# The first item of the gate projection ahead of the last Strassen product

## The chip, the core and the metric

The kernel runs on one core of a Trainium2 chip. The metric is the device time of one execution in microseconds (us), lower is better. The core has a matmul engine (PE, with its weight loads as PEld), a vector engine (DVE), a scalar engine (ACT), GpSimd (POOL) and a queue for DMA issues (SP). Each engine works its own instructions in the order in which the program lists them and waits for the others by semaphores.

## What is computed

One decoder layer on a sequence of 1024 tokens with 1024 channels, all in float32. What matters here is the order of the stages:

```python
h = layer_norm(x)
u, b_gate, c_gate, z_a, z_s, xbc, dt_raw, g_a, g_s = split(h @ w_in)     # the large projection
y_a = silu(z_a) * b_gate * causal_conv3(c_gate * u)
y_a = y_a @ w_a_out                                                      # "a" items
y_s = gated_group_rmsnorm(ssd(xbc, dt) + d_skip * xs, z_s) @ w_s_out     # "s" items
mixed = sigmoid(g_a) * y_a + sigmoid(g_s) * y_s
h = layer_norm(alpha * h + mixed @ w_o)
```

## The kernel before

Every product is made from float32 split in a high and a low part (`hi`, `lo`), as three matmuls: hi by hi, hi by lo, lo by hi. A row group is a block of 128 rows of the transposed input weight, so 128 output channels. The large projection takes two row groups at a time as a pair, and makes each pair by seven products of half size (a Strassen scheme); the pairs are numbered 0 to 43, the products 1 to 7. The last pairs, 40 to 43, hold the gates g_s.

The work of PE is one list, `items`, written out by hand, and one loop over it (L1069) issues each item with all that belongs to it on the other engines. An item `("p", p, j)` is product j of pair p: 12 matmuls of 128x512, four slices of the inner dimension by three. An item `("a", j, kh)` is half of the inner dimension of output block j of the gate projection (`y_a @ w_a_out`, whose result is multiplied by sigmoid(g_a)): 24 matmuls, 12 into each of two PSUM banks. The items `("s", g, j)` follow. Within a pair the products come as 1, 2, 6, 5, 7, 4, and product 3 is put off until after product 1 of the next pair. After the last pair there is no next one, so its product 3 stands right behind its product 4, and then the `a` items begin.

The loop prepares weights ahead: at item n ACT makes the `hi` of item n+3 (`prep_hi`, L288), DVE the `lo` of item n+2 (`prep_lo`, L105 by way of `sub_split`), and SP loads raw weights up to item n+5. `lo` tiles have three buffers and `hi` tiles four, so each waits until PE is through with an older item. PSUM results are added up one item later: what `sums` holds for item n+1 is put on DVE behind the weight preparation of that item (L1029). Everything from item 21 on is pinned: each engine keeps the order in which the loop wrote it.

Three banks matter. Products 5 and 3 of a pair accumulate in the bank `c4`, in one tile. Between the two, DVE has to add the partial sum to the second row group (`add(obh, C4[p], obl)` of product 7, one item later); product 3 may only begin after that. Product 4 uses the bank `cx`, and DVE empties it by `add(obl, ps, obl)` one item later. `pbank` gives the `a` items their banks in turn, and the first that it gives, to the item ("a", 0, 0), is `cx`.

The operands of the `a` items are the eight blocks of y_a. They are loaded (`ya`) when the scan is done, and `turn_ya(k)` splits block k into high and low for both halves of the tokens: two ACT copies (L818), one subtraction on DVE and one on POOL (L105, tiles `a_k0` and `a_k1`). Blocks 0 to 5 are turned in the last pair's items 2, 6, 5, 7, 4 and 3, blocks 6 and 7 in the item ("a", 0, 0), ahead of that item's `sums`:

```python
elif kind == "a":
    item_a(i, j, hi, lo)
    if i == 0 and j == 0:
        turn_ya(6)
        turn_ya(7)
...
for f in sums.pop(n, ()):
    f()
```

("a", 0, 0) reads blocks 0 to 3, ("a", 0, 1) blocks 4 to 7. `prep_y(t)` loads and scales the operands of the `s` items (`gt`, `rb`); `y_at` says at which item. The tile `sga0` of the first `a` item (sigmoid(g_a), loaded by SP) lies where the first output of pair 43 (`oa43`) was, `sga1` where the second was (`ob43`), and SP can issue those two loads only when ACT has stored `oa43` and `ob43` (L586, L587) to `sgs_d`.

Of the kernel before, what the change touches and what calls it, by code (L numbers as in the profile page):

```python
# [28 lines left out]
KT = D // P  # L29
# [16 lines left out]
def trunk_kernel(ctx: ExitStack, tc: tile.TileContext, x, w_in, w_dt, w_a, w_s, w_o, par, con,  # L46
# [148 lines left out]
    items = [("p", p, j) for j in (1, 2, 3, 6, 5, 7, 4) for p in range(EARLY)]  # L195
    late = None
    for p in range(EARLY, NP):
        items += [("p", p, 1)] + ([late] if late else []) + [("p", p, j) for j in (2, 6, 5, 7, 4)]
        late = ("p", p, 3)
    items.append(late)  # L200
    items += [("a", j, kh) for j in range(KT) for kh in range(2)]
    WAVE = 3
    s_order = [(g, j) for gs in ((0, 1), (2, 3)) for j in range(WAVE) for g in gs]
    s_order += [(g, j) for j in range(WAVE, KT) for g in range(G)]
# [662 lines left out]
    a0, s0 = item_at["a", 0, 0], item_at["s", 0, 0]  # L867
    y_at = {}
    for t, i in enumerate((1, 3, 5, 6, 8, 10, 11, 13, 14, 15, 16, 17, 18, 19, 19, 20)):
        y_at.setdefault(a0 + i, []).append(t)  # L870

    SG = [("x", 5), ("x", 6), ("x", 4), ("c", 0), ("c", 0), ("o", 2), ("o", 3), ("o", 1)]
    gy_at = {s0 + 5: 0, s0 + 7: 1, s0 + 9: 2}
# [389 lines left out]
```

## Time and profile before

| | |
|---|---|
| time, median of 3 runs | 1408.17 us (1406.65 to 1409.61) |
| the profiled execution | 1411.06 us, of which the span of the trace is 1408.9 us |
| mean granted clock of PE over the span | 0.992 |
| PE busy | 98% of the span |
| DVE, ACT, POOL busy | 69%, 50%, 34% |
| last product of pair 43 (product 3) | first matmul at 1038.83 us of the span |
| first `a` item | first matmul at 1042.24 us |

Times in the trace are counted from the start of the span. A row of the timeline gives the start, the duration, the engine, the line of the kernel, the operation with its tiles (numbers in tile names are left out, so `p` is any product's bank), the shape and a count; in brackets stands how long the engine sat idle ahead of it, and what is thought to have released it.

### The profile page before, as it was taken

The numbers are of one execution on the slowest core, as the hardware profiler recorded it, in microseconds if no ns is written. First come the engines' busy times: TensorE is split into PE (matmuls) and PEld (weight loads), VectorE is DVE, ScalarE is ACT, GpSimd is POOL, SyncE is SP. The second block draws the span as 40 slices with busy tenths as digits, with TensorE's granted clock in tenths as the row PEclk, the third lists the DMA queues.
The fourth block names the chain that finished last, engine by engine and source line by source line (L and its number), as shares of the span: only waits on it lengthen the run. The fifth ranks groups of instructions, "written<-read, shape, count | busy, mean of one in ns | idle before, by whom it ended". The sixth has DMA issues, their size and how long they took to land.

```text
span 1408.9 us, 18441 instructions
## 1 busy us (share of the span) xinstructions
PE 1378.9 (98%) x6532; PEld 1110.0 (79%) x6532; DVE 975.2 (69%) x1422; ACT 701.7 (50%) x1228; POOL 485.3 (34%) x367
## 2 busy tenths in 40 slices
PE   8799999999999999999999999999999999999997
PEld 5577887888888888888888888888878888888886
DVE  8867779787779878688878686867464463224766
ACT  4565565656567555566566565555452231113431
POOL 1312215453435444334444343444230000000487
PEclk9899999999999999999999999999999999999999
DMA  6022363564454555544555445543457763223422
GB/s 239 16 76 94 115 145 110 129 180 129 141 134 133 153 155 147 131 131 130 151 157 187 132 154 127 153 128 127 172 174 269 232 222 139 100 75 110 144 90 90
DMA packets 166459, 198.09 MB, mean 141 GB/s; under 512 B 10688, under 2 KB 116064, under 8 KB 166368
## 3 DMA queue, kind: packets, MB, share of 16 engines
q1 hardware_dynamic: 158160, 167.14, 40.9%
q10 hardware_dynamic: 8208, 29.79, 5.3%
q8 instruction: 51, 0.84, 0.2%
q14 instruction: 40, 0.33, 0.1%
HBM read 146.28 MB, written 50.61 MB: 140 GB/s over the span
## 4 chain that ended last, share of the span: by engine, by line
PE 91%; DVE 4%; issue 2%; ACT 1%; POOL 1%; DMA 0%; ACTq 0%; POOLq 0%; DVEq 0%
PE p L1020 11%; PE p L1021 11%; PE p L1022 11%; PE pU L1020 8%; PE pU L1022 8%; PE pU L1021 8%; PE p_ws L859 4%; PE p_ws L860 4%; PE p_ws L861 4%; PE ya L691 2%; PE st L696 2%; PE p_wa L859 2%; PE p_wa L860 2%; PE p_wa L861 2%; PE p_wo L1157 2%
## 5 line engine op out<-in xcount | busy, mean ns | idle before, releaser
L105 DVE TENSOR_TENSOR wlop<-raw_a,whip 128x512 fp32r<-128x512 f32 x210 | 185.0, 881 | 160.5 <-ACT whip L288 64.7
L1020 PE MATMUL p<-b,whip 128*128 128x512 f32 x352 | 143.8, 409 | 7.6 <-ACT whip L286 4.8
L1020 PE MATMUL pU<-t,whip 128*128 128x512 f32 x352 | 145.2, 414 | 0.0
L1020 PE MATMUL p<-t,whip 128*128 128x512 f32 x352 | 142.0, 403 | 0.0
L1021 PE MATMUL p<-b,whip 128*128 128x512 f32 x352 | 140.4, 399 | 0.0
L1022 PE MATMUL p<-b,wlop 128*128 128x512 f32 x352 | 139.8, 398 | 0.0
L1021 PE MATMUL pU<-t,whip 128*128 128x512 f32 x352 | 139.3, 396 | 0.0
L1022 PE MATMUL p<-t,wlop 128*128 128x512 f32 x352 | 139.1, 395 | 0.0
L1021 PE MATMUL p<-t,whip 128*128 128x512 f32 x352 | 139.1, 395 | 0.0
L1022 PE MATMUL pU<-t,wlop 128*128 128x512 f32 x352 | 139.0, 395 | 0.0
L676 POOL TENSOR_TENSOR xw<-xd,dte_t 128x256 f32<-128x256 f32 x56 | 46.9, 837 | 260.5 <-DVE xd L662 260.5
L288 ACT ACTIVATE whip<-raw_a 128x512 fp32r<-128x512 f32 x207 | 125.8, 622 | 19.2 <-issue 10.5
L942 POOL TENSOR_TENSOR res<-res,ag 128x1024 f32<-128x1024 f32 x8 | 19.7, 2464 | 276.1 <-ACT res L941 276.1
L239 POOL TENSOR_TENSOR s<-raw_a,raw_a 128x512 f32<-128x512 f32 x42 | 69.6, 1657 | 92.1 <-DVE wlop L105 87.8
L860 PE MATMUL p_ws<-y,whis 128*128 128x512 f32 x256 | 100.9, 394 | 0.0
L859 PE MATMUL p_ws<-y,whis 128*128 128x512 f32 x256 | 100.8, 394 | 0.0
L861 PE MATMUL p_ws<-y,wlos 128*128 128x512 f32 x256 | 100.7, 393 | 0.0
L105 DVE TENSOR_TENSOR wlos<-raw_s,whis 128x512 fp32r<-128x512 f32 x32 | 22.1, 692 | 113.0 <-PE p_ws L861 89.2
L253 POOL TENSOR_TENSOR raw_a<-raw_a,s 128x512 f32<-128x512 f32 x42 | 67.5, 1606 | 90.2 <-issue 78.7
L105 DVE TENSOR_TENSOR wlop<-s,whip 128x512 fp32r<-128x512 f32 x84 | 80.2, 966 | 13.2 <-PE p L1022 8.5
L1020 PEld LDWEIGHTS p<-b,whip 128*128 128x128 f32 x352 | 67.0, 190 | 23.7 <-ACT whip L286 5.1
L288 ACT ACTIVATE whis<-raw_s 128x512 fp32r<-128x512 f32 x32 | 20.3, 634 | 129.6 <-PE p_ws L860 109.0
(225 smaller groups left out, 3404.7 us busy)
## 6 DMA issues: line engine op xcount, KB each, us to landing
raw_a<-in_w_in_dram SPq DMA_DIRECT2D x168, 256.0 KB, 4.0
em<-cum_d SPq DMA_DIRECT2D x64, 256.0 KB, 6.8
xg_d<-cv ACTq DMA_DIRECT2D x16, 512.0 KB, 7.0
xT<-xg_d SPq DMA_DIRECT2D x32, 256.0 KB, 4.7
z<-zs_d SPq DMA_DIRECT2D x32, 256.0 KB, 3.1
gat_d<-y SPq DMA_DIRECT2D x32, 256.0 KB, 2.8
gt<-gat_d SPq DMA_DIRECT2D x16, 512.0 KB, 6.4
raw_s<-in_w_s_dram SPq DMA_DIRECT2D x32, 256.0 KB, 4.3
```

The source lines that it names most:

```text
L105: return eng.tensor_tensor(lo, full, hi.bitcast(F32), ALU.subtract)
L239: fs = [lambda: Gp.tensor_tensor(s1, r["a21"], r["a22"], ALU.add), lambda: Gp.tensor_tensor(s2, s1, r["a11"], ALU.subtract), lambda: Gp.te ...
L253: f = lambda: Gp.tensor_tensor(a12, a12, s1s[p]["s2"], ALU.subtract)
L288: S.activation(flat(hi), src, AF.Copy)
L676: Gp.tensor_tensor(xw, XD[n, i], dte_t[:, hs, c].unsqueeze(2).to_broadcast([P, HG, HD]), ALU.mult)
L691: PE.matmul(YA[n][o:o + HD, t * P:(t + 1) * P], lhsT=XD[n, i][:, h, :], rhs=EM[n, i][:, h, :], start=True, stop=True)
L859: PE.matmul(ps, lhsT=hi[:, k, :], rhs=u[:, 0, :], start=start, stop=False)
L860: PE.matmul(ps, lhsT=hi[:, k, :], rhs=u[:, 1, :], start=False, stop=False)
L861: PE.matmul(ps, lhsT=lo[:, k, :], rhs=u[:, 0, :], start=False, stop=stop)
L1020: PE.matmul(ps, lhsT=hi[:, k, :], rhs=u[:, 0, :], start=first, stop=False, skip_group_check=True)
L1021: PE.matmul(ps, lhsT=hi[:, k, :], rhs=u[:, 1, :], start=False, stop=False, skip_group_check=True)
L1022: PE.matmul(ps, lhsT=lo[:, k, :], rhs=u[:, 0, :], start=False, stop=(k == 3), skip_group_check=True)
```

## The change

The item ("a", 0, 0) changes places with the last product 3. The loads of y would come one item earlier with it, since they are counted from that item; one is added, so they stay where they were.

```diff
-    items.append(late)
-    items += [("a", j, kh) for j in range(KT) for kh in range(2)]
+    items += [("a", 0, 0), late] + [("a", j, kh) for j in range(KT) for kh in range(2)][1:]
...
-        y_at.setdefault(a0 + i, []).append(t)
+        y_at.setdefault(a0 + 1 + i, []).append(t)
```

The changed kernel has one line less, so every line behind the change has a number lower by one.

On PE, at the end of pair 43: `p4_43_9497` is the bank of product 4 (`cx`), `p4_43_9446` that of products 5 and 3 (`c4`), `p_wa0_0` and `p_wa0_1` are the two banks of the first output block of the `a` items, the first of them `cx` again. Of each run of matmuls the first or the last stands here. Before:

```order
L1022 MATMUL p4_43_9497<-t4_3_694,wlop43_4_9444 128x512
L1020 MATMUL p4_43_9446<-b22_0_499,whip43_3_9442 128x512
L1022 MATMUL p4_43_9446<-b22_3_529,wlop43_3_9469 128x512
L859 MATMUL p_wa0_0_9550<-a_00_9406,whia0_0_9467 128x512
L859 MATMUL p_wa0_1_9563<-a_01_9407,whia0_0_9467 128x512
L859 MATMUL p_wa0_0_9550<-a_40_9511,whia0_1_9493 128x512
```

With the change:

```order
L1021 MATMUL p4_43_9497<-t4_3_694,wlop43_4_9444 128x512
L858 MATMUL p_wa0_0_9525<-a_00_9408,whia0_0_9442 128x512
L858 MATMUL p_wa0_1_9538<-a_01_9409,whia0_0_9442 128x512
L1019 MATMUL p4_43_9446<-b22_0_499,whip43_3_9467 128x512
L1021 MATMUL p4_43_9446<-b22_3_529,wlop43_3_9495 128x512
L858 MATMUL p_wa0_0_9525<-a_40_9511,whia0_1_9493 128x512
```

The 24 matmuls of the first `a` item now stand between product 4 and product 3, and the item that opens `cx` anew comes directly behind the one that filled it.

On DVE, at the same place: `ob43<-p4_43_9446` is the add that lets product 3 begin, `ob43<-p4_43_9497` the add that empties `cx`, `a_k0` the subtraction for block k of y_a, `wlo...` the low part of a weight. Before:

```order
L105 TENSOR_TENSOR a_20_9459<-ya2_9279,a_20_9459 128x512
L105 TENSOR_TENSOR wlop43_3_9469<-raw43_a12_9219,whip43_3_9442 128x512
L105 TENSOR_TENSOR a_30_9485<-ya3_9281,a_30_9485 128x512
L105 TENSOR_TENSOR wloa0_0_9495<-raw_a0_0_9412,whia0_0_9467 128x512
L1029 TENSOR_TENSOR ob43_9471<-p4_43_9446,ob43_9471 128x512
L105 TENSOR_TENSOR a_40_9511<-ya4_9283,a_40_9511 128x512
L105 TENSOR_TENSOR wloa0_1_9521<-raw_a0_1_9440,whia0_1_9493 128x512
L1029 TENSOR_TENSOR ob43_9471<-p4_43_9497,ob43_9471 128x512
L105 TENSOR_TENSOR a_50_9536<-ya5_9285,a_50_9536 128x512
L105 TENSOR_TENSOR wloa1_0_9546<-raw_a1_0_9465,whia1_0_9519 128x512
L105 TENSOR_TENSOR a_60_9576<-ya6_9287,a_60_9576 128x512
L105 TENSOR_TENSOR a_70_9582<-ya7_9289,a_70_9582 128x512
```

With the change:

```order
L105 TENSOR_TENSOR a_20_9459<-ya2_9279,a_20_9459 128x512
L105 TENSOR_TENSOR wloa0_0_9469<-raw_a0_0_9385,whia0_0_9442 128x512
L105 TENSOR_TENSOR a_30_9485<-ya3_9281,a_30_9485 128x512
L105 TENSOR_TENSOR wlop43_3_9495<-raw43_a12_9219,whip43_3_9467 128x512
L1028 TENSOR_TENSOR ob43_9471<-p4_43_9446,ob43_9471 128x512
L105 TENSOR_TENSOR a_40_9511<-ya4_9283,a_40_9511 128x512
L105 TENSOR_TENSOR wloa0_1_9521<-raw_a0_1_9440,whia0_1_9493 128x512
L105 TENSOR_TENSOR a_60_9551<-ya6_9287,a_60_9551 128x512
L105 TENSOR_TENSOR a_70_9557<-ya7_9289,a_70_9557 128x512
L1028 TENSOR_TENSOR ob43_9471<-p4_43_9497,ob43_9471 128x512
L105 TENSOR_TENSOR wloa1_0_9568<-raw_a1_0_9465,whia1_0_9519 128x512
L105 TENSOR_TENSOR a_50_9582<-ya5_9285,a_50_9582 128x512
```

The subtractions of blocks 6 and 7 now stand ahead of the add that empties `cx`, and that of block 5 behind it. The two weights of the exchanged items have changed places.

On ACT, behind the first `a` items: `oa43` and `ob43` are the two gates of pair 43, then stored to `sgs_d6` and `sgs_d7`; `y_00` and `y_01` are the first operands of the `s` items, made from the load `gt0`. Before:

```order
L586 ACTIVATE oa43_9354<-oa43_9354 128x1024
L587 DMA sgs_d6_71<-oa43_9354 128x1024
L288 ACTIVATE whia2_0_9593<-raw_a2_0_9517 128x512
L586 ACTIVATE ob43_9471<-ob43_9471 128x1024
L587 DMA sgs_d7_72<-ob43_9471 128x1024
L288 ACTIVATE whia2_1_9629<-raw_a2_1_9542 128x512
L818 ACTIVATE y_00_9664<-gt0_9623 128x512
L818 ACTIVATE y_01_9665<-gt0_9623 128x512
```

With the change:

```order
L585 ACTIVATE oa43_9354<-oa43_9354 128x1024
L586 DMA sgs_d6_71<-oa43_9354 128x1024
L287 ACTIVATE whia2_1_9627<-raw_a2_1_9564 128x512
L817 ACTIVATE y_00_9662<-gt0_9620 128x512
L817 ACTIVATE y_01_9663<-gt0_9620 128x512
L585 ACTIVATE ob43_9471<-ob43_9471 128x1024
L586 DMA sgs_d7_72<-ob43_9471 128x1024
```

The second gate and its store now come behind the first two operands of the `s` items. On SP one thing moves: the load of `sga0` stands ahead of the load of `raw_a2_1`, no longer behind it.

## The prediction

> **What bounds the kernel now.** I read the page first, for the engine that carries the end, then the list of PE's waits, then the timelines of PE, DVE, POOL and ACT around the exchanged items. The page's first rows of engine shares and of the chain that ended last:
>
> ```profile
> PE 1378.9 (98%) x6532; PEld 1110.0 (79%) x6532; DVE 975.2 (69%) x1422; ACT 701.7 (50%) x1228; POOL 485.3 (34%) x367
> ...
> PE 91%; DVE 4%; issue 2%; ACT 1%; POOL 1%; DMA 0%; ACTq 0%; POOLq 0%; DVEq 0%
> ```
>
> PE is the bound almost throughout, so a microsecond in which PE stands still is a microsecond of the time, and other engines matter only where PE waits for them. Three of the thirteen rows of PE's waits:
>
> ```profile
> PE p L1020 <- ACT whip L286: 4.8, 1, 4.8
> ...
> PE p L1020 <- ACT a L818: 2.1, 1, 2.1
> ...
> PE p_wa L859 <- DVE ob L1029: 0.4, 1, 0.4
> ```
>
> The first lies near the start (at 55 us) and serves below as a measure. The second and third lie at the place of the change. The timeline of PE there:
>
> ```profile
> 1036.36 0.40 PE L1022 MATMUL p<-t,wlop 128*128 128x512 f32 x1
> 1038.83 0.47 PE L1020 MATMUL p<-b,whip 128*128 128x512 f32 x1 [2.07 <-ACT a L818]
> 1039.14 0.39 PE L1021 MATMUL p<-b,whip 128*128 128x512 f32 x1
> ...
> 1041.47 0.40 PE L1022 MATMUL p<-b,wlop 128*128 128x512 f32 x1
> 1042.24 0.47 PE L859 MATMUL p_wa<-a,whia 128*128 128x512 f32 x1 [0.37 <-DVE ob L1029]
> ```
>
> Product 4 of pair 43 ends at 1036.76. PE then idles 2.07, does product 3, idles 0.37, and starts the first `a` item at 1042.24. From 1039.14 to 1041.47 are ten steps, so a matmul costs 0.233. What PE waited for is seen on DVE:
>
> ```profile
> 1033.37 1.79 DVE L105 TENSOR_TENSOR a<-ya,a 128x512 fp32r<-128x512 f32 x1
> ...
> 1036.29 1.79 DVE L105 TENSOR_TENSOR wloa<-raw_a,whia 128x512 fp32r<-128x512 f32 x1
> 1038.00 0.68 DVE L1029 TENSOR_TENSOR ob<-p,ob 128x512 f32<-128x512 f32 x1
> 1038.60 1.17 DVE L105 TENSOR_TENSOR a<-ya,a 128x512 fp32r<-128x512 f32 x1
> 1039.69 1.80 DVE L105 TENSOR_TENSOR wloa<-raw_a,whia 128x512 fp32r<-128x512 f32 x1
> 1041.41 0.68 DVE L1029 TENSOR_TENSOR ob<-p,ob 128x512 f32<-128x512 f32 x1
> ...
> 1043.21 2.40 DVE L105 TENSOR_TENSOR a<-ya,a 128x512 fp32r<-128x512 f32 x2
> 1045.54 0.68 DVE L1029 TENSOR_TENSOR oa<-p,oa 128x512 f32<-128x512 f32 x1
> ```
>
> DVE works here without a gap and is behind. The add that lets product 3 begin ends at 1038.68, and PE starts 0.15 later; the name that the row gives as releaser is an ACT copy that happened to end then, and product 3 reads nothing of it. The add that empties `cx` ends at 1042.09, and PE starts the first `a` item, whose first bank is `cx`, again 0.15 later. The chain of waits goes the same way at this place, by DVE:
>
> ```profile
> 1038.00 0.68 DVE ob L1029
> ...
> 1039.69 1.80 DVE wloa L105
> 1041.49 0.61 DVE ob L1029
> ```
>
> So there are two adds, and each frees one item. Before, the item that needs the early add comes first. The change turns that round: the `a` item, which needs the late add, goes first, and product 3, which could run from 1038.83 on, stands behind it in PE's queue.
>
> **The change, term by term.** All is measured against the start of the first `a` item, 1042.24, ahead of which product 3 was done.
>
> *The late add comes later still.* The order on DVE shows the subtractions of blocks 6 and 7 in front of it, because they are written in the `a` item and its `sums` come after. This pair took 2.40 in the row of 1043.21, and the next operation began 2.33 after it: I take 2.33. The ends: two operations at the step of a lone one (1038.00 to 1038.60, 0.60) give 1.2; two at the step of the slow rows (1039.69 to 1041.41, 1.72) give 3.4. The slow ones run beside POOL:
>
> ```profile
> 1035.71 5.24 POOL L105 TENSOR_TENSOR a<-ya,a 128x512 fp32r<-128x512 f32 x3 [1.09 <-ACT a L818]
> 1043.46 3.32 POOL L105 TENSOR_TENSOR a<-ya,a 128x512 fp32r<-128x512 f32 x2 [2.52 <-ACT a L818]
> ```
>
> POOL's queue now has blocks 6 and 7 right behind 4, so it works on to about 1042.7 (four at 5.24/3); the first of the two subtractions at 1041.41 still meets it, the second hardly. That is the mixture of the 2.40 row. The `a` item would start at 1042.24 + 2.33 = 1044.57.
>
> *Product 3 loses its place inside the wait.* Its 12 matmuls, 12 x 0.233 = 2.80, were done while PE would have waited for the late add anyway. Behind the `a` item they cost their full length: 2.80. Of this I am surest; it has one answer.
>
> *The clock.* PE now idles from 1036.76 to 1044.57, 7.8 us in one piece, where it idled 2.07 and 0.37. What a long idle time does is seen after the 4.82 us at the start of the program:
>
> ```profile
> 55.12 0.80 PE L1020 MATMUL p<-b,whip 128*128 128x512 f32 x1 [4.82 <-ACT whip L286]
> 55.71 0.63 PE L1021 MATMUL p<-b,whip 128*128 128x512 f32 x1
> ...
> 61.26 0.40 PE L1020 MATMUL p<-b,whip 128*128 128x512 f32 x1
> 50.00:60.00 10.00, 5.18 (x15) 3.84 (x14) 9.96 (x13) 4.58 (x8) 4.40 (x3) 0.55 0.17 52
> 60.00:70.00 10.00, 10.00 (x42) 8.04 (x41) 8.63 (x16) 6.07 (x11) 0.00 (x0) 0.94 0.01 2
> ```
>
> The last two rows give the granted clock (third number from the end) as 0.55 and 0.94. From 55.12 to 61.26 are 14 steps; at 0.233 they take 3.27, here 6.14. The loss is 2.87, and I take it. At 2.07 idle the steps were 0.233 at once, so the lower end is 0. The upper: the two windows together were at half speed for about 9.0 + 1.2 = 10.2 us; if all of that fell on matmuls the loss would be near 4.6. [...]
>
> *ACT's order.* The high part of the `a` weight moves up by one place, to where the high part for product 3 was made:
>
> ```profile
> 1028.59 3.05 SPq L228 DMA_DIRECT2D raw_a<-in_w_a_dram  x6
> DMA to landing us min/median/max: 3.4/5.8/9.0
> 1031.42 0.62 ACT L288 ACTIVATE whip<-raw_a 128x512 fp32r<-128x512 f32 x1
> 1031.95 1.13 ACT L818 ACTIVATE a<-ya 128x512 fp32r<-128x512 f32 x2
> 1032.99 0.61 ACT L288 ACTIVATE whia<-raw_a 128x512 fp32r<-128x512 f32 x1
> ...
> 1037.09 0.62 ACT L288 ACTIVATE whia<-raw_a 128x512 fp32r<-128x512 f32 x1
> ```
>
> Its raw weight is the first of the six loads issued from 1028.59. It had landed by 1032.99, where its copy began without an idle gap; by the shortest landing, 3.4, not before 1031.99. So ACT now waits 0.6 to 1.6 at 1031.42, and everything behind it on ACT shifts. DVE feels it at its subtraction of 1033.37, which would be ready at 1033.1 to 1034.1: 0 to 0.8. I take 0.3. The rest of ACT's shift is covered by DVE's backlog.
>
> *What moves and costs nothing.* The weights of the exchanged items change places on DVE, same shape, both done by 1038.1. The subtraction of block 5 and its POOL half now wait for ACT's copy behind `whia1_1`, which needs a buffer of the first `a` item; but the next item that reads block 5 comes a whole product 3 (2.80) after that item, and copy and subtraction take 0.6 + 1.1 + 0.7. On SP one raw load now stands behind `sga0`; its item is six places on. These stay covered as long as PE is the later one. The loads of y stay at their items.
>
> *Sum.* 2.33 + 2.80 + 2.87 + 0.3 = 8.3. The profiled execution took 1411.06 with a span of 1408.9, 2.9 above the median of the runs; the terms don't depend on that, so I add to the median: 1408.17 + 8.3 = 1416.5.
>
> **The rivals.**
>
> *No fall of the clock.* Then 2.33 + 2.80 + 0.3 = 5.4, 1413.6. The row of 2.07 speaks for it, the row of 4.82 against it.
>
> *A new stall behind the queue of SP.* Later stages had slack, and the change takes some: `sga0` can be loaded only after `oa43` is stored, and everything else that SP issues waits behind it.
>
> ```profile
> 1047.34 0.33 ACTq L587 DMA_DIRECT2D sgs_d<-oa  x1
> 1050.90 0.33 SPq L880 DMA_DIRECT2D sga<-sga_d  x1
> 1059.72 1.28 DVE L848 SCALAR_TENSOR_TENSOR gt<-gt,par_t,rb 128x1024 f32<-128x1024 f32 x1 [3.77 <-DMA gt<-gat_d]
> 1042.24:1047.84 5.60, 5.60 (x24) 4.56 (x25) 3.93 (x5) 3.25 (x6) 3.32 (x2) 1.00 0.01 3
> ```
>
> From the store to the load 3.56, from there to DVE's work on `gt0` 8.8; an `a` item takes 5.60. With E the end of product 3: two DVE operations (1.4) and the gate (1.1) bring the store to E + 2.6, `sga0` to E + 6.2, `gt0` on DVE to E + 15.0 and 1.28 more. Now the second gate stands behind the two copies of y (1.2): gate 1.1, store and load 3.6, so `sga1` is issued near E + 22.3, and `gt1` done by E + 22.3 + 8.8 + 1.3 = E + 32.4. Behind that on DVE stands the low part (0.7) for an item that begins at E + 6 x 5.6 = E + 33.6. That is half a microsecond of slack, by a landing price from a crowded queue. If it fails, it costs up to 2: 1418.5 with the middle value.
>
> *DVE at its lone rate.* If POOL didn't slow DVE, each subtraction would step 0.6; the four ACT copies of blocks 6 and 7, behind the copy of 1037.09 at the step of the pair of 1031.95 (0.52), would end near 1039.8, the add near 1040.6, and PE start at 1040.75. Then the change costs 1040.75 + 2.80 - 1042.24 = 1.3, 1409.5, within what can be told. Against it: POOL's work is all still there.
>
> *The other side: the item hides the wait.* If the `a` item could start right at 1036.76, the early add would be long done when product 3 comes, and 2.07 + 0.37 = 2.44 would go: 1405.7. For that `cx` would have to be empty at 1036.8. It is decided at the late add: it would have to end before 1039.4 (1042.24 - 2.80) for any gain, and it ended at 1042.09 with two fewer operations in front of it. Only another first bank would do it, and the 0.37 row shows that the bank is `cx`.
>
> **How the numbers follow.** The forecast has 0.60, no fall of the clock 0.15, the stall 0.12, the lone rate 0.08, the other side 0.05. A change under 0.2% (2.8 us) can't be told from none here. The forecast, the first rival and the stall are slower: 0.87, and of the lone rate some, since a clock fall could come on top: 0.90. The other side is mostly within 0.2%: faster 0.02, same 0.08. The range begins at 1411.8, just under the cheap ends of all terms (1.2 + 2.80 + 0 + 0 = 4.0), and ends at 1420.5, near the forecast with the slow pair (3.4), 0.8 on ACT and the dear clock (4.6), 11.6, less what hardly comes together, or with the stall on top.
>
> **What the profile after would show.** PE without product 3 in the gap: last matmul of product 4, then one idle time of about 7.8 us in front of the first `p_wa`, released by the DVE add of `ob`; two DVE subtractions on `a` ahead of that add; steps of about 0.43 for some 6 us and then 0.233; product 3 behind 24 `p_wa` matmuls without a wait; no other PE wait in the `a` items. I am wrong if the first `p_wa` starts before 1041, if the steps behind the idle time are 0.233 at once, or if PE waits for a weight at the fifth or sixth item further on.

## The result, and the profile after

The changed kernel took 1417.41 us (median of 4 runs, 1416.37 to 1418.81) against 1408.08 before (4 runs, 1406.65 to 1409.61): 9.3 us slower by the medians, where 8.3 was forecast. The ratio on record is 1.0059, 95% interval 1.0046 to 1.0071; it is not the ratio of the medians (1.0066) and stands for 8.3 us, from 6.5 to 10.0. Its profiled execution took 1417.01, with a span of 1415.0.

The page's row of engine shares, after the change, shows the same work on every engine as before. The time that came on top is time without work, or with slower work:

```profile
PE 1379.1 (97%) x6532; PEld 1113.1 (79%) x6532; DVE 977.8 (69%) x1422; ACT 700.6 (50%) x1228; POOL 485.1 (34%) x367
```

To find the place, I cut both spans at two events that both programs have: the end of product 4 of pair 43, and the first matmul of the first `s` item. Between them lie product 3 and all 16 `a` items. The rows give the stretch, its length, the busy time and count of PE, PEld, DVE, ACT and POOL, the granted clock, the DMA share and GB/s. Before:

```profile
1036.76:1131.91 95.15, 92.71 (x396) 74.47 (x397) 48.73 (x64) 26.49 (x44) 7.50 (x5) 1.00 0.67 228
1131.91:1408.91 277.00, 267.47 (x1177) 216.98 (x1175) 136.53 (x203) 68.13 (x102) 73.91 (x32) 0.99 0.35 119
```

After:

```profile
1034.30:1138.02 103.72, 95.16 (x397) 76.73 (x397) 49.02 (x64) 25.79 (x45) 7.91 (x5) 0.95 0.58 192
1138.02:1415.02 277.00, 267.48 (x1177) 217.27 (x1175) 137.37 (x205) 68.80 (x104) 73.92 (x32) 0.99 0.36 125
```

The stretch with the change in it grew by 103.72 - 95.15 = 8.57, at a mean clock of 0.95 where it was 1.00. What follows it takes 277.00 in both: nothing is lost or won behind the place. The 8.57 is what the rest of this document takes apart; the 0.8 by which the medians differ more stays open. The spans differ by only 6.1, because the profiled execution of before lost 2.46 ahead of the place, where both programs do the same (last section).

Inside the stretch one wait of PE is new. Its row in the list of PE's waits after the change (total, times, longest), where it is the largest:

```profile
PE p_wa L858 <- DVE ob L1028: 8.6, 1, 8.6
```

The timeline of PE shows the gap, the slow matmuls behind it, and product 3 (L1019 to L1021 on `p`) behind the `a` item. A row is start, duration, engine, line, operation, and the idle time before it with its releaser:

```profile
1033.90 0.40 PE L1021 MATMUL p<-t,wlop 128*128 128x512 f32 x1
1042.86 0.77 PE L858 MATMUL p_wa<-a,whia 128*128 128x512 f32 x1 [8.56 <-DVE ob L1028]
1043.42 0.63 PE L859 MATMUL p_wa<-a,whia 128*128 128x512 f32 x1
...
1048.89 0.40 PE L860 MATMUL p_wa<-a,wloa 128*128 128x512 f32 x1
...
1051.22 0.40 PE L1019 MATMUL p<-b,whip 128*128 128x512 f32 x1
...
1054.02 0.40 PE L858 MATMUL p_wa<-a,whia 128*128 128x512 f32 x1
```

From 1042.86 to 1048.89 are 14 steps; at 0.233 they would take 3.27, here they took 6.03, at a granted clock of 0.51, which is 2.76 more. Product 3 runs from 1051.22 to 1054.02 without a wait, its full 2.80.

DVE after the change, the rows that answer to those shown of before:

```profile
1031.75 0.69 DVE L105 TENSOR_TENSOR a<-ya,a 128x512 fp32r<-128x512 f32 x1 [0.76 <-ACT a L817]
...
1036.38 0.68 DVE L1028 TENSOR_TENSOR ob<-p,ob 128x512 f32<-128x512 f32 x1
1036.99 1.17 DVE L105 TENSOR_TENSOR a<-ya,a 128x512 fp32r<-128x512 f32 x1
1038.08 1.75 DVE L105 TENSOR_TENSOR wloa<-raw_a,whia 128x512 fp32r<-128x512 f32 x1
1039.76 2.36 DVE L105 TENSOR_TENSOR a<-ya,a 128x512 fp32r<-128x512 f32 x2
1042.04 0.68 DVE L1028 TENSOR_TENSOR ob<-p,ob 128x512 f32<-128x512 f32 x1
```

The early add ends at 1037.06. Product 3 could have started then; nothing takes it up, since PE's queue now holds the `a` item in front. The pair of subtractions (1039.76) stands ahead of the late add, which ends at 1042.72; PE starts 0.14 later. The chain of waits follows just this, DVE first and then PE:

```profile
1038.08 1.75 DVE wloa L105
1039.83 2.28 DVE a L105 x2
1042.11 0.61 DVE ob L1028
...
1042.86 0.77 PE p_wa L858
```

### The profile page after: what moved, and what is told of

Same layout as the page of the kernel before. It is cut to its first block, busy times and chain, and to the rows that moved or that the text cites. A ratio compares the mean times of both kernels' runs of the same rounds, so it can differ in the third digit from the quotient of the medians.

```text
span 1415.0 us, 18438 instructions
## 1 busy us (share of the span) xinstructions
PE 1379.1 (97%) x6532; PEld 1113.1 (79%) x6532; DVE 977.8 (69%) x1422; ACT 700.6 (50%) x1228; POOL 485.1 (34%) x367
## 4 chain that ended last, share of the span: by engine, by line
PE 91%; DVE 4%; issue 2%; ACT 1%; POOL 1%; DMA 0%; ACTq 0%; POOLq 0%; DVEq 0%
PE p L1019 11%; PE p L1020 11%; PE p L1021 11%; PE pU L1019 8%; PE pU L1021 8%; PE pU L1020 8%; PE p_ws L859 4%; PE p_ws L860 4%; PE p_ws L858 4%; PE ya L690 2%; PE p_wa L858 2%; PE p_wa L859 2%; PE p_wa L860 2%; PE st L695 2%; PE p_wo L1156 2%
## 5 line engine op out<-in xcount | busy, mean ns | idle before, releaser
L1019 PE MATMUL p<-b,whip 128*128 128x512 f32 x352 | 143.5, 408 | 5.5 <-ACT whip L285 4.8
L1019 PE MATMUL pU<-t,whip 128*128 128x512 f32 x352 | 145.0, 413 | 0.0
L1019 PE MATMUL p<-t,whip 128*128 128x512 f32 x352 | 142.1, 404 | 0.0
L1021 PE MATMUL p<-b,wlop 128*128 128x512 f32 x352 | 139.5, 397 | 0.0
L1021 PE MATMUL p<-t,wlop 128*128 128x512 f32 x352 | 139.3, 396 | 0.0
L1021 PE MATMUL pU<-t,wlop 128*128 128x512 f32 x352 | 139.2, 396 | 0.0
L641 ACT ACTIVATE em<-em,cum_t 128x128 f32<-128x128 f32 x256 | 81.3, 390 | 6.5 <-ACT ob L585 3.6
L1019 PEld LDWEIGHTS p<-b,whip 128*128 128x128 f32 x352 | 66.9, 190 | 21.0 <-ACT whip L285 5.1
```

The lines of the kernel that those rows point to most:

```text
L641: S.activation(em[:, h, :], em[:, h, :], AF.Relu, bias=cum_t[:, 8 * g + 4 * i + h, c:c + 1], scale=-1.0)
L1019: PE.matmul(ps, lhsT=hi[:, k, :], rhs=u[:, 0, :], start=first, stop=False, skip_group_check=True)
L1021: PE.matmul(ps, lhsT=lo[:, k, :], rhs=u[:, 0, :], start=False, stop=(k == 3), skip_group_check=True)
```

## The experiments

The ratios are against the kernel before on the same chip; they are not ratios of the medians, and differ from those by up to 0.0005. There were two chips: on the first (the first four kernels) before took 1408.45 (15 runs), on the second (the last two) 1409.93 (14 runs). "The stretch" is the one cut above, from one profile of each kernel: 95.15 before, 103.72 after. What follows it took 276.99 to 277.01 in all eight profiles. What lies ahead of it, the same matmuls in all, took from 1032.15 to 1036.76. So the terms are read from the stretches. The medians say the same more coarsely: measured from before, the two differ by 0.1 to 1.5 us, and for the last kernel by 2.5.

**Another first bank.** The changed kernel, with `cx` moved from the first to the last place among the banks that the `a` items open (the list is read from its second entry on). One `yy` moves up to the first place, and one `U` takes the place that it left. Then the first `a` item needs no late add. If the bank is the cause, the whole loss goes; if it is a queue or the order of weights, it stays.

```diff
-        return bank(("U", "cx", "yy", "tr", "U", "c4", "yy", "st")[n_bank[0] % 8], name)
+        return bank(("cx", "yy", "yy", "tr", "U", "c4", "U", "st")[n_bank[0] % 8], name)
```

> The changed kernel, with the banks of the later projections handed out in another turn, so that the first a item opens two yy banks and not cx. Theory A (PE waits for cx, which the add of product 4 empties late): PE goes from product 4 to the a item without an idle gap, product 3 finds the early add done, the waits of 2.07 and 0.37 us are gone; a wait up to 0.5 us may appear in the second a item for block 5 of y_a. 1405.7 to 1406.2 us, ratio 0.998 to 0.999, no slow clock there. Rival B (the loss lies behind the place: the second gate and the load of sga0 and sga1 hold up SP and DVE): those are unchanged, the loss stays, about 1414 to 1417. Rival C (the a item waits for its operands, y_a or weights, which ACT, DVE and POOL make late, not for the bank): idle time and loss stay, 1417.

Measured: 1406.51 (11 runs), 0.9988 (0.9980 to 0.9997); the stretch took 93.11. The timeline of PE of this kernel:

```profile
1032.03 0.40 PE L1021 MATMUL p<-t,wlop 128*128 128x512 f32 x1
1032.27 0.39 PE L858 MATMUL p_wa<-a,whia 128*128 128x512 f32 x1
...
1037.87 0.39 PE L1019 MATMUL p<-b,whip 128*128 128x512 f32 x1
...
1042.37 0.50 PE L859 MATMUL p_wa<-a,whia 128*128 128x512 f32 x1 [0.61 <-DVE a L105]
```

The `a` item follows product 4 in the next step, product 3 follows it, and both gaps of before are gone as well. On DVE of the same kernel the late add still stands behind the pair, only PE doesn't wait for it:

```profile
1037.60 2.40 DVE L105 TENSOR_TENSOR a<-ya,a 128x512 fp32r<-128x512 f32 x2
1039.92 0.68 DVE L1028 TENSOR_TENSOR ob<-p,ob 128x512 f32<-128x512 f32 x1
```

So the loss hangs on one thing: the first bank of the moved item is the one that waits for the late add. With another bank the same order is 2.04 shorter in the stretch than before. What is left is one wait of 0.61 for the subtraction of a later block. The other bank in the order of before wasn't run; by the rows of before it would take away the 0.37 and leave the 2.07, since there product 3 comes first and waits for the early add.

**The two subtractions behind the adds.** The changed kernel, with blocks 6 and 7 written after the sums of the first `a` item. This takes the pair from in front of the late add.

```diff
             item_a(i, j, hi, lo)
-            if i == 0 and j == 0:
-                turn_ya(6)
-                turn_ya(7)
...
         for f in later.pop(n, ()):
             f()
+        if (kind, i, j) == ("a", 0, 0):
+            turn_ya(6)
+            turn_ya(7)
```

> The changed kernel, with the turning of blocks 6 and 7 put behind the add that empties cx, on all engines. Theory A: PE's idle time shrinks by the two DVE subtractions, from 8.6 to 6.3 us; product 3 and the slow clock cost what they did: 1415.1 us. Rival B and C: no change of the idle time by more than 0.5 us, 1417.

Measured: 1413.55 (4 runs), 1.0039 (1.0025 to 1.0053); the stretch 101.00. PE's wait in this kernel:

```profile
1041.79 0.76 PE L858 MATMUL p_wa<-a,whia 128*128 128x512 f32 x1 [6.16 <-DVE ob L1028]
```

The idle time fell from 8.56 to 6.16, by 2.40, and the slow matmuls cost 2.45 instead of 2.76: together 2.7, the 2.72 of the stretch. Of the 2.40, 0.12 is not the pair: DVE's wait for ACT further up was 0.64 here and 0.76 after the change. The pair ahead of the add is worth what its own 2.28 says.

**The gap filled.** The changed kernel, with 32 matmuls put into an unused bank ahead of the first `a` item; their result isn't used. PE is busy in the gap, so the clock should hold if the idle time is what lowers it, while the late add comes no sooner.

```diff
+        if j == 0 and kh == 0:
+            idle = bank("st", "idle")
+            for k in range(32):
+                PE.matmul(idle, lhsT=hi[:, k % 4, :], rhs=B["b22", k % 4][:, 0, :], start=True, stop=True)
```

> The changed kernel with 32 matmuls of 128x512 into an unused bank in front of the first a item, 7.5 us of work whose result is not used. Theory A: PE still starts the a item when the add is done, but with a gap under 1.5 us instead of 8.6, and at full clock at once: 2.8 us less than the changed kernel, 1414.6. If the slow steps have another cause than the idle time, the time stays at 1417.4; if the added matmuls stretch the path, it is longer.

Measured: 1415.38 (4 runs), 1.0052 (1.0037 to 1.0068); the stretch 100.78, that is 2.94 less than after with 32 matmuls more. PE's timeline:

```profile
1033.93 0.40 PE L1025 MATMUL p<-t,wlop 128*128 128x512 f32 x1
1034.17 7.63 PE L883 MATMUL idle<-b,whia 128*128 128x512 f32 x32
1042.61 0.50 PE L858 MATMUL p_wa<-a,whia 128*128 128x512 f32 x1 [0.81 <-DVE ob L1032]
1042.94 0.40 PE L859 MATMUL p_wa<-a,whia 128*128 128x512 f32 x1
1043.18 0.40 PE L860 MATMUL p_wa<-a,wloa 128*128 128x512 f32 x1
```

The `a` item starts 8.68 after the last matmul of product 4 (1033.93 to 1042.61), only 0.28 sooner than after the change (1033.90 to 1042.86), but its matmuls step at 0.24 or less from the second on, and the granted clock of the stretch is 1.00, where it was 0.95. This parts the clock's term from the wait: of the 2.94, 0.28 is the earlier start and 2.66 the steps. The medians differ by less, 1415.38 against 1417.41.

**The two subtractions in the old order.** The kernel before, with blocks 6 and 7 written in product 3's item, ahead of its sums: the pair alone, without the exchange.

```diff
             item_p(i, j, hi, lo)
+            if (i, j) == (NP - 1, 3):
+                turn_ya(6)
+                turn_ya(7)
...
             item_a(i, j, hi, lo)
-            if i == 0 and j == 0:
-                turn_ya(6)
-                turn_ya(7)
```

> The kernel before, with the turning of blocks 6 and 7 moved one item up, in front of the add that empties cx; items in the old order. Theory A: product 3 still runs inside the wait; the a item starts 2.3 us later, so PE idles 2.1 and 2.7 us: 1410.4 us, and up to 1.7 more if the clock falls in the gap of 2.7. That would show the first term alone, without the loss of product 3's cover. Rival B: as before, 1408.

Measured: 1414.01 (4 runs), 1.0045 (1.0031 to 1.0059); the stretch 100.92, 5.77 more than before. A miss in size: at most 1412.1 was expected. PE's timeline and DVE's pair:

```profile
1036.66 0.47 PE L1020 MATMUL p<-b,whip 128*128 128x512 f32 x1 [2.05 <-DVE ob L1029]
...
1043.48 0.76 PE L859 MATMUL p_wa<-a,whia 128*128 128x512 f32 x1 [3.79 <-DVE ob L1029]
```

```profile
1039.26 3.47 DVE L105 TENSOR_TENSOR a<-ya,a 128x512 fp32r<-128x512 f32 x2
```

Here the pair delayed the next operation by 3.40, not 2.33: POOL worked through both subtractions.

```profile
1033.56 8.62 POOL L105 TENSOR_TENSOR a<-ya,a 128x512 fp32r<-128x512 f32 x5 [1.10 <-DMA raw_a<-in_w_a_dram]
```

The gap in front of the first `a` item grew from 0.37 to 3.79, and the 12 slow steps behind it (5.26, 0.44 each instead of 0.233) cost 2.46: 3.4 + 2.5, the measured 5.8 within 0.1. The expectation had 2.3 for the pair and at most 1.7 for the clock; the 1.7 was my estimate, which no run shows. The first row also settles a name: product 3 waits for the add of `ob`, as the prediction read it, and not for the ACT copy that the profile of before named.

**Another bank, and block 5 earlier.** The first experiment's order of banks, and the subtraction of block 5 moved from product 3's item to the first `a` item, ahead of blocks 6 and 7. This is aimed at the 0.61 that was left.

```diff
             if i == 0 and j == 0:
-                turn_ya(6)
-                turn_ya(7)
+                for k in (5, 6, 7):
+                    turn_ya(k)
...
-            if i == NP - 1 and j in (2, 6, 5, 7, 4, 3):
+            if i == NP - 1 and j in (2, 6, 5, 7, 4):
                 assert not micro
-                turn_ya((2, 6, 5, 7, 4, 3).index(j))
+                turn_ya((2, 6, 5, 7, 4).index(j))
```

> The kernel with the other first banks, and block 5 of y_a turned in the first a item, ahead of blocks 6 and 7, no longer in the item of product 3, where its ACT copy stood behind a weight that waits for PE. Theory A: the wait of 0.6 us in the second a item for block 5 is gone and nothing takes its place; 0.5 to 0.6 us less than other_bank, 1405.9 us, ratio 0.998. Rival: the DVE add that empties cx and the weight behind it come 0.6 to 1.7 us later and a wait for the weight of the third a item appears instead: same as other_bank.

Measured: 1405.53 (8 runs), 0.9973 (0.9963 to 0.9983), faster than both kernels. Its stretch:

```profile
1033.77:1126.00 92.23, 92.23 (x396) 74.28 (x396) 47.67 (x61) 24.83 (x43) 7.90 (x5) 1.00 0.63 205
```

PE is busy for 92.23 of 92.23 at a granted clock of 1.00: no wait of PE is left at this place. Against before the stretch is 2.92 shorter and the runs 4.4; the other 1.5 is not in the stretch and stays open (before itself was 1.5 higher on this chip). The stretch is 0.88 shorter than with the other bank alone, the wait of 0.61 and what it cost at its ends. The medians of these two kernels can't be set against each other, since they come from different chips.

**The high parts in the old order.** The changed kernel, with the high parts of the two exchanged items made on ACT in the order of before, so that ACT doesn't stand waiting for the `a` weight.

```diff
-            prep_hi(n + LA)
+            swap = {a0: a0 + 1, a0 + 1: a0}
+            prep_hi(swap.get(n + LA, n + LA))
```

> The changed kernel with ACT's order for the two exchanged items as before: the high part for product 3 made first, that of the a item second. Theory A: the 1.5 us for which ACT waited for the raw weight of the a item go, DVE's gap of 0.76 in front of block 2 goes, PE's idle time shrinks from 8.6 to about 7.8 us: 1416.6 us. If ACT's wait does not reach DVE's add, the idle time stays at 8.6 us and the time at 1417.4.

Measured: 1413.84 (6 runs, 1412.83 to 1417.28), 1.0033 (1.0021 to 1.0045); the stretch 101.56. PE's timeline:

```profile
1039.83 0.76 PE L858 MATMUL p_wa<-a,whia 128*128 128x512 f32 x1 [7.68 <-DVE ob L1028]
...
1042.94 0.39 PE L859 MATMUL p_wa<-a,whia 128*128 128x512 f32 x1
```

The idle time fell by 0.88, so ACT's wait is the cause of that much. The other 1.28 of the 2.16 in the stretch is the clock: only 7 slow steps (3.11, 0.44 each) instead of 14 (6.03, 0.43 each), behind an idle time of nearly the same length. The time was expected at 1416.6 and is 2.8 lower. Against before on its chip it is 3.9 longer, where the stretch is 6.41 longer; this is not explained. The six runs spread over 4.5 us. That the number of slow matmuls changes from run to run would explain the spread, but the runs that were only timed have no records of it; that is argued, not shown.

## Why the prediction was right, step by step

- *The mechanism.* The early add frees product 3, the late add frees `cx`, and the exchange puts the item that needs the late one first. The experiment with another bank shows this, and refutes the rival that some queue or weight was the cause.
- *The pair ahead of the late add*, 2.33: the chain has 2.28, and its removal took 2.40 from the idle time, 0.12 of it by a shorter wait for ACT. In the old order the same pair took the other bound, 3.40, because there POOL's queue reached further: to 1042.18, with the pair from 1039.26 and the next operation at 1042.66; after the change it reached to 1040.97, with the pair from 1039.76 and the next operation at 1042.04.
- *Product 3 uncovered*, 2.80: its 12 matmuls took 2.80 behind the `a` item, and none of them stands in the gap.
- *The clock*, 2.87: 2.76 after the change. With the gap filled by matmuls 2.66 of the stretch went with the slow steps, so the rival without a fall of the clock is out, for this gap. That the clock falls was right; that the size fits within 0.11 is in part luck. The 2.87 was read from one row, the wait of 4.82 near the start in the profile of before. Behind the same wait the kernel with the change lost only 1.78 (9 steps in 3.88); the mean granted clock from 48 to 75 us was 0.87 there and in the five other profiles with a wait of 4.8, where the profile of before had 0.81. At the place itself the idle times of 3.79 to 8.56 lost 1.48 to 2.76.
- *ACT's order*, 0.3: this step was mis-sized. ACT waited 1.50 for its raw weight, near the late end of the bounds (0.6 to 1.6), and DVE felt 0.76, near the end of its bound (0.8); 0.88 went when the order was restored. The two rows, of ACT and of DVE after the change:

```profile
1030.56 0.63 ACT L287 ACTIVATE whia<-raw_a 128x512 fp32r<-128x512 f32 x1 [1.50 <-DMA raw_a<-in_w_a_dram]
1031.75 0.69 DVE L105 TENSOR_TENSOR a<-ya,a 128x512 fp32r<-128x512 f32 x1 [0.76 <-ACT a L817]
```

- *The sum*: 2.28 + 2.80 + 2.76 + 0.76 = 8.6 against 8.57 in the stretch, where 8.3 was forecast, and the time 1417.41 against 1416.5; the idle time 8.56 against 7.8, which was reckoned without ACT's term; that term's 0.76 is the difference.
- *The stall behind SP's queue* did not come: no other PE wait stands in the `a` items, and the rest takes 277.00. The price of the rival was also too high. With E = 1054.02, the end of product 3, SP and DVE after the change:

```profile
1059.31 0.33 SPq L879 DMA_DIRECT2D sga<-sga_d  x1
...
1074.78 0.32 SPq L879 DMA_DIRECT2D sga<-sga_d  x1
```

```profile
1082.00 1.29 DVE L847 SCALAR_TENSOR_TENSOR gt<-gt,par_t,rb 128x1024 f32<-128x1024 f32 x1 [2.37 <-DMA gt<-gat_d]
1083.20 0.68 DVE L105 TENSOR_TENSOR wloa<-raw_a,whia 128x512 fp32r<-128x512 f32 x1
```

  `sga0` was issued at E + 5.3 (forecast 6.2), `sga1` at E + 20.8 (22.3), `gt1` done at E + 29.3 (32.4). The low part ended at 1083.9, its item began at E + 33.6: a slack of 3.7, where I had 0.5.
- *DVE at its lone rate* is refuted for this place: the subtractions beside POOL still step at 1.7, and POOL works as forecast, from 1034.36 without a gap:

```profile
1034.36 6.61 POOL L105 TENSOR_TENSOR a<-ya,a 128x512 fp32r<-128x512 f32 x4 [0.74 <-DMA raw_a<-in_w_a_dram]
```

- *The other side* carried its right condition: only another first bank would do it. It was forecast at 1405.7 if the bank were empty, and with another bank the kernel took 1406.51.
- *The loads of y*, which I left at nothing: they are counted from the first `a` item, which moved up by one, and with the one that was added they stay at the items they had. A kernel without that addition wasn't run, so this rests on the 277.00 and on PE's waits alone.

## What to carry to other kernels

When an item is moved up in a hand-written order, ask first which PSUM bank it opens, and which operation empties that bank; here the `a` item started 0.14 to 0.15 us after that operation was done, at the old place in the list as at the new. Work written in the same item ahead of that operation stands ahead of it in its engine's queue too. And count an idle time of several us on PE higher than its length: at this place each of 3.8 to 8.6 us cost another 1.5 to 2.8 in slow matmuls. Another order of the same banks turned +9.3 us into -1.9.

## What the runs showed of the hardware

Behind nearly the same idle time the clock fell in one profile and held in seven. Near 216 us PE waits 2.23 to 2.24 in all eight profiles, for the same operation (`em`, on DVE). In the profile of before the following matmuls ran slow (the windows' row of 214 to 226, granted clock 0.86):

```profile
214.00:226.00 12.00, 9.76 (x48) 7.38 (x47) 10.41 (x10) 4.82 (x9) 8.34 (x5) 0.86 0.30 84
```

In the profile after they didn't, as in the other six (granted clock 1.00 in each):

```profile
214.00:226.00 12.00, 9.77 (x53) 7.53 (x52) 11.93 (x11) 7.27 (x15) 7.43 (x5) 1.00 0.31 90
```

From the first matmul behind that wait to the first at full speed it took 3.89 there (217.88 to 221.77) and 2.39 after the change (216.90 to 219.29). This is 1.5 of the 2.46 that the profiled execution of before lost ahead of the place. The other 1.0 arose in the slow matmuls near the start of the program (mean granted clock from 48 to 75 us 0.81, after the change 0.87). Behind the wait of 4.82 they lasted 6.14 there, by the rows in the prediction, and 3.88 after the change:

```profile
55.20 0.80 PE L1019 MATMUL p<-b,whip 128*128 128x512 f32 x1 [4.82 <-ACT whip L285]
...
59.08 0.40 PE L1020 MATMUL p<-b,whip 128*128 128x512 f32 x1
```

Nor does the time of the slow steps (0.43 to 0.44 each, at full speed 0.233) go by the length of the idle time. At the place 8.56 idle was followed by 6.03 slow, 7.68 by 3.11, 6.16 by 5.25, and 3.79 by 5.26; near the start the same 4.82 was followed by 6.14 before and by 3.88 after the change. What sets the time of the slow steps, these rows don't show.
